# A feed-forward whose up projection goes by Strassen's block product and whose down projection goes in six groups

## The chip, the cores and the metric

The kernel is one program on one core of a Trainium2 chip. The metric is the device time of one execution in microseconds (us); each kernel is run several times and the median is given. PE is the matrix engine, DVE, ACT and POOL are the vector, scalar and general engines, SP issues the DMAs, all on one queue.

## The reference

Two trunk layers of width 1024 run over 640 tokens: 512 latent tokens (y_sample) and 128 context tokens (y_prompt), with shared weights. Each layer is a mixer of four branches (window attention, latent attention, pooling, gated delta rule) with a residual, and then a gated feed-forward:

```python
mod = jnp.matmul(jax.nn.silu(cond), lp['w_mod']) + lp['b_mod']
sh1, sc1, ga1, sh2, sc2, ga2 = jnp.split(mod[:, None, :], 6, axis=-1)
...
x = x + ga1 * rmsnorm(mix, lp['g_post1'])
h2 = rmsnorm(x, lp['g_pre2']) * (1 + sc2) + sh2
gt, up = jnp.split(jnp.matmul(h2, lp['w_up']), 2, axis=-1)
f = jnp.matmul(jax.nn.silu(gt) * up, lp['w_down'])
x = x + ga2 * rmsnorm(f, lp['g_post2'])
```

w_up is 1024 x 5632 (2816 gate and 2816 up columns), w_down 2816 x 1024. The change touches the three lines from h2 to f and what stands beside them in time.

## The kernel before, in words

All data are fp32. A product is made of two parts, hi (rounded to the matmul's format) and lo (the rest), and of three matmuls, hi x hi, hi x lo and lo x hi. Weights are split as they arrive: wchunk (L137) loads a tile of 128 x 1024 into "raw", ACT copies it to "whi" (L144) and DVE subtracts to get "wlo" (L145).

The activations h lie feature by token in hhi and hlo, 8 blocks of 128 features by 640 tokens, in two token halves of 384 and 256. The up projection takes 128 weight columns at a time (up_chunk, L1243): 8 blocks x 3 matmuls x 2 halves = 48 matmuls. There are 22 gate and 22 up chunks in a layer. ACT makes the Silu of the gate (L1291), DVE multiplies the up product in (L1293) and splits the result (L162).

The down projection goes in three groups of 8, 7 and 7 column blocks (FGROUPS) and two halves of 512 output columns, 660 matmuls of 512 columns in a layer. The sums of a group are added to y, in the tiles "acc" and "oh". The last half of the last group goes token tile by token tile (21 matmuls each): behind each tile stands post (L1219). It multiplies by the gate vector into a tile of "tg" (L1227), computes the norm's factor, adds both halves to the residual x in a tile of "V" with two scalar_tensor_tensor (L1232, L1233) and stores it (L1234). x was loaded into V beforehand (x_load, L1185); V, "tg", "cv" and "dt" have two buffers each. For layer 0 the tile then goes on into prenorm (L355), the norm that makes h of the next layer: transposes on PE, DVE scaling into P, hi on ACT (L378), lo on POOL or DVE (L380).

At the start of each feed-forward the norms of the last token tiles are late. ffn_head (L1246) runs four weight chunks over the first 384 tokens meanwhile.

In layer 0's feed-forward a filler computes the next layer's modulation (mod_group_v, L299) on DVE: 96 weight tiles of 128 x 512 with two operations each (L313, L315), whose raw tiles alternate between "dt" and "cv". step() issues one tile at a time between chunks.

Each engine runs its instructions in one fixed order, which a scheduler sets from the program's order and priorities when the kernel is built. An instruction that waits holds all behind it on its engine. Tiles of a tag share that tag's buffers, so a new tile waits until the readers of an old one are done.

Of the kernel before, what the change touches and what calls it, by code (L numbers as in the profile page):

```python
# [26 lines left out]
FGROUPS = ((0, 8), (8, 15), (15, 22))  # L27
# [77 lines left out]
class Step:  # L105
    def __init__(self, nc, tc, pools, I, O):
        self.nc, self.tc, self.I, self.O = nc, tc, I, O
        self.sb, self.psp, self.dr = pools
        self.n = 0
        self.late = []  # L110
        self.dma = nc.sync
        self.bg = None
# [5 lines left out]
    BUFS = dict(raw=2, whi=3, wlo=3, acc=4, tg=2, cv=2, oh=4, X=2, T=2, U=4, V=2, P=4, dt=2, st=4)  # L118
# [180 lines left out]
    def mod_group_v(self, M, g, bank, tr_tag):  # L299

        nc, I, l = self.nc, self.I, M["l"]
        pb = self.ps(bank)
        accs = []
        for j in range(4):
            acc = self.t("P", [128, SLOT])[:, :1024].rearrange("p (s c) -> p s c", s=2)
            accs.append(acc)
            for k in range(KT):
                raw = self.t("cv", [128, TG])[:, :512] if k % 2 else self.t("dt", [128, 512])
                c = g * 2048 + j * 512
                self.dma.dma_start(raw, I["w_mod"][l, k * 128:k * 128 + 128, c:c + 512])  # L310
# [12 lines left out]
        yield  # L323
# [31 lines left out]
    def prenorm(self, i, x, M, which, hh):  # L355
# [13 lines left out]
        for q in range(2):  # L369
# [849 lines left out]
    def post(self, i, t0, t1, s, G, xsrc, xdst, M, which, hh2):  # L1219
# [15 lines left out]
        if hh2 is not None:  # L1235
            norm = lambda: self.prenorm(i, x, M, which, hh2)
            if i < 3:
                norm()
            else:
                self.late.append(norm)  # L1240


    def up_chunk(self, l, c0, tags=("whi", "wlo")):  # L1243
        return self.wchunk([(slice(0, 128), self.I["w_up"][l][:, c0:c0 + 128].rearrange("(k p) c -> p k c", p=128))], KT, 128, tags)

    def ffn_head(self, l, hh):  # L1246

        head = {}
        for j, (n, up) in enumerate(((0, 0), (0, 1), (1, 0), (1, 1))):
            ch = self.up_chunk(l, up * D_FF + n * 128, ("whi", "wlo") if j < 3 else ("oh", "oh"))  # L1250
            p = self.ps("s" if up else "g")[:, :HV[0][1]]
            self.fm_h(ch, hh, outs=[p, None], halves=(0,))
            head[n, up] = ch, p
            if j in (0, 1):
                self.late.pop(0)()
        return head

    def ffn(self, l, hh, head, M, Mn, xsrc, xdst, hh2, filler):
        step = lambda: next(filler, None) if filler is not None else None
# [3 lines left out]
        G = None  # L1263
        for gi, (f0, f1) in enumerate(FGROUPS):
            nf = f1 - f0
            parts = {}
            for nm in ("hi", "lo"):
                if nm == "hi":
                    tl = [self.t("X", [128, 2 * SLOT], F32R)[:, :2560].rearrange("p (a t) -> p a t", a=4) for _ in range(2)]
                else:  # L1270
                    tl = [self.t(tg, [128, SLOT], F32R)[:, :1280].rearrange("p (a t) -> p a t", a=2)
                          for tg in ("T", "T", "U", "U")]
                per = 4 if nm == "hi" else 2
                parts[nm] = [tl[n // per][:, n % per, :] for n in range(nf)]
            for n in range(nf):
                gu = []
                for up in range(2):
                    bank = "s" if up else "g"
                    if gi == 0 and (n, up) in head:
                        ch, p = head[n, up]  # L1280
                        outs = [p, self.ps(bank)[:, :HV[1][1]]]
                        self.fm_h(ch, hh, outs=outs, halves=(1,))
                    else:
                        outs = self.fm_h(self.up_chunk(l, up * D_FF + (f0 + n) * 128), hh, bank)
                    gu.append(outs)
                    if n < nf - 1:
                        step()
                gp, up = gu
                s = self.t("tg", [128, TG])[:, :NTOK]
                for p, (o, sz) in zip(gp, HV):  # L1290
                    nc.scalar.activation(s[:, o:o + sz], p, AF.Silu)  # L1291
                for p, (o, sz) in zip(up, HV):
                    nc.vector.tensor_tensor(s[:, o:o + sz], s[:, o:o + sz], p, op=ALU.mult)  # L1293
                self.split(parts["hi"][n], parts["lo"][n], s)
            hs = (lambda k: parts["hi"][k], lambda k: parts["lo"][k])
            kc = [(k, min(k + 2, nf)) for k in range(0, nf, 2)]
            last = gi == len(FGROUPS) - 1
            for half in range(2):
                co = half * 512
                mk = lambda a, b: self.wchunk([(slice(0, 512), wd[:, f0 + a:f0 + b, co:co + 512])], b - a, 512)  # L1300
                if gi == 0 and half == 0:
                    for i in range(NT):
                        if i < 4:
                            ys.append(self.t("acc", [128, SLOT])[:, :1024])
                        else:
                            ys.append(self.t("oh", [128, SLOT])[:, :1024])
                if last and half == 1:
                    G = self.load_G(M, 1)
                    for i in range(NT):
                        y = ys[i][:, :512]  # L1310
                        nc.gpsimd.tensor_tensor(y, y, G[0 if i < 4 else 1][:, 0:512], op=ALU.mult)  # L1311
                    chs = [mk(a, b) if b - a == 2 else self.wchunk1(wd[:, f0 + a:f0 + b, co:co + 512]) for a, b in kc]
                    for i in range(NT):
                        p = self.ps("g")
                        for ci, (a, b) in enumerate(kc):
                            self.tmm(p, chs[ci], range(b - a), hs, range(a, b), i, ci == 0, ci == len(kc) - 1)
                        y = ys[i]
                        nc.vector.tensor_tensor(y[:, 512:], y[:, 512:], p, op=ALU.add)
                        self.post(i, y[:, :512], y[:, 512:], self.ffs[i], G, xsrc, xdst, Mn, 0, hh2)
                else:  # L1320
# [12 lines left out]
                    if last:  # L1333
                        self.ffs = []
                        for i in range(NT):
                            s = self.t("o_s2", [128, 2], bufs=6)
                            j = self.t("tg", [128, TG])[:, :NTOK]
                            nc.scalar.activation(j[:, :512], ys[i][:, :512], AF.Square, accum_out=s[:, 0:1])  # L1338
                            self.ffs.append(s)


    def run(self):
# [29 lines left out]
        for l in range(DEPTH):  # L1372
# [42 lines left out]
            hh = self.new_h()  # L1415
# [44 lines left out]
```

## Time and profile before

| | us |
|---|---|
| median of 3 runs (2438.87 to 2442.44) | 2440.92 |
| the profiled execution | 2436.05 |
| its span | 2433.9 |
| PE busy in it | 2349.3 (97%) |
| DVE busy | 1351.3 (56%) |
| ACT busy | 833.6 (34%) |
| POOL busy | 270.2 (11%) |

The mean granted clock of PE was 0.992 of full speed. Busy times of engines overlap, and matmuls are pipelined: the time from one start to the next is the price of one, not its length. In the records an idle time before an instruction stands in brackets with what ended it.

### The profile page before, as it was taken

How to read it: one execution, taken by the hardware profiler on the slowest of the kernel's cores; microseconds unless marked ns; L12 is line 12 of the kernel's file. 1: busy time of each engine (PE TensorE's matmuls, PEld its weight loads, DVE VectorE, ACT ScalarE, POOL GpSimd, SP SyncE). 2: the span in 40 equal slices, each digit the busy share in tenths (PEclk: the TensorE clock that was granted, in tenths of full speed). 3: DMA queues.
4: the chain of work that ended last, by engine and by line, in shares of the span. 5: the costliest groups of instructions: out<-in, count | busy, mean ns of one | idle time of the engine just before them, and what ended most of it. 6: DMA issues, size and time to landing. Idle time of an engine off the chain costs nothing.

```text
span 2433.9 us, 38640 instructions
## 1 busy us (share of the span) xinstructions
PE 2349.3 (97%) x15350; PEld 2084.1 (86%) x15350; DVE 1351.3 (56%) x2920; ACT 833.6 (34%) x1682; POOL 270.2 (11%) x324
## 2 busy tenths in 40 slices
PE   7999999999998999999989999999999999999998
PEld 5877688989877989989969777898898799899996
DVE  5562788576358746473285647874764553223225
ACT  3341554232235222212264534522422442222222
POOL 0000203132031000000020011221311200000001
PEclk9999999999999999999999999999999999999999
DMA  8637123424445636352243121242353332222223
GB/s 258 162 122 228 40 75 97 107 59 114 137 135 170 185 113 190 111 168 74 77 128 100 29 63 54 88 109 76 88 164 99 120 122 78 87 78 70 78 74 100
DMA packets 361668, 269.45 MB, mean 111 GB/s; under 512 B 72128, under 2 KB 312384, under 8 KB 361488
## 3 DMA queue, kind: packets, MB, share of 16 engines
q1 hardware_dynamic: 361488, 266.98, 37.4%
q8 instruction: 121, 1.98, 0.3%
q14 instruction: 59, 0.48, 0.1%
HBM read 234.73 MB, written 32.20 MB: 110 GB/s over the span
## 4 chain that ended last, share of the span: by engine, by line
PE 77%; DVE 11%; DMA 4%; ACT 3%; issue 2%; POOL 1%; SPq 1%; DVEq 0%; ACTq 0%; POOLq 0%
PE psg L129 39%; PE pss L129 24%; PE pso L129 4%; PE psc L129 4%; PE pst L129 2%; PE pst L134 2%; DVE wlo L145 1%; DVE P L990 1%; DVE P L989 1%; ACT whi L144 1%; PE psc L212 1%; DMA V<-in_w_mod 1%; DMA tg<-gd 1%; POOL acc L1177 1%; DMA gd<-tg 0%
## 5 line engine op out<-in xcount | busy, mean ns | idle before, releaser
L129 PE MATMUL psg<-hhi,whi 128*128 128x384 f32 (+1 forms) x2144 | 683.6, 319 | 13.4 <-ACT hhi L378 6.6
L129 PE MATMUL psg<-hlo,whi 128*128 128x384 f32 (+1 forms) x2144 | 681.5, 318 | 3.8 <-POOL hlo L380 3.8
L129 PE MATMUL psg<-hhi,wlo 128*128 128x384 f32 (+1 forms) x2144 | 679.0, 317 | 2.2 <-DVE wlo L145 2.0
L145 DVE TENSOR_TENSOR wlo<-raw,whi 128x1024 fp32r<-128x1024 f32 (+1 forms) x260 | 320.3, 1233 | 458.5 <-ACT whi L144 455.6
L144 ACT ACTIVATE whi<-raw 128x1024 fp32r<-128x1024 f32 (+1 forms) x260 | 272.3, 1049 | 672.2 <-PE psg L129 289.9
L129 PEld LDWEIGHTS psg<-hhi,whi 128*128 128x128 f32 x2144 | 406.2, 189 | 30.2 <-issue 8.4
L129 PEld LDWEIGHTS psg<-hlo,whi 128*128 128x128 f32 x2144 | 406.4, 190 | 20.3 <-issue 13.4
L129 PEld LDWEIGHTS psg<-hhi,wlo 128*128 128x128 f32 x2144 | 406.8, 190 | 12.9 <-issue 6.6
L129 PE MATMUL pss<-hhi,wlo 128*128 128x384 f32 (+1 forms) x672 | 208.1, 310 | 0.0
L129 PE MATMUL pss<-hhi,whi 128*128 128x384 f32 (+1 forms) x672 | 208.1, 310 | 0.0
L129 PE MATMUL pss<-hlo,whi 128*128 128x384 f32 (+1 forms) x672 | 208.1, 310 | 0.0
L1293 DVE TENSOR_TENSOR tg<-tg,pss 128x384 f32<-128x384 f32 (+1 forms) x88 | 42.8, 486 | 159.9 <-PE pss L129 159.9
L129 PEld LDWEIGHTS pss<-hhi,wlo 128*128 128x128 f32 x672 | 126.5, 188 | 0.0
L129 PEld LDWEIGHTS pss<-hlo,whi 128*128 128x128 f32 x672 | 126.5, 188 | 0.0
L129 PEld LDWEIGHTS pss<-hhi,whi 128*128 128x128 f32 x672 | 126.4, 188 | 0.0
L129 PE MATMUL psg<-oh,whi 128*128 128x384 f32 (+1 forms) x512 | 119.8, 317 | 4.8 <-DVE tg L1175 4.5
L1144 ACT ACTIVATE tg<-psg 128x384 f32<-128x384 f32 (+1 forms) x128 | 54.9, 431 | 188.9 <-PE psg L129 170.4
L1177 POOL TENSOR_TENSOR acc<-acc,tg 128x640 f32<-128x640 f32 x48 | 83.4, 1741 | 243.4 <-DVE tg L1175 243.3
L1311 POOL TENSOR_TENSOR acc<-acc,oh 128x512 f32<-128x512 f32 x8 | 12.8, 1602 | 857.5 <-ACT tg L1338 857.5
L129 PEld LDWEIGHTS psg<-oh,whi 128*128 128x128 f32 x512 | 85.3, 188 | 13.4 <-DVE tg L1175 8.4
L129 PE MATMUL psg<-wlo,X 128*128 128x512 f32 x224 | 88.8, 397 | 0.0
L129 PE MATMUL psg<-whi,X 128*128 128x512 f32 x224 | 87.5, 394 | 0.0
(488 smaller groups left out, 3985.5 us busy)
## 6 DMA issues: line engine op xcount, KB each, us to landing
raw<-in_w_up SPq DMA_DIRECT2D x88, 512.0 KB
raw<-in_w_in SPq DMA_DIRECT2D x86, 512.0 KB
raw<-in_w_down SPq DMA_DIRECT2D x40, 512.0 KB
V<-in_w_mod SPq DMA_DIRECT2D x32, 512.0 KB
cv<-in_w_mod SPq DMA_DIRECT2D x48, 256.0 KB
dt<-in_w_mod SPq DMA_DIRECT2D x48, 256.0 KB
raw<-in_w_o SPq DMA_DIRECT2D x16, 512.0 KB
xs<-V SPq DMA_DIRECT2D x15, 512.0 KB
```

The lines of the kernel that those rows point to most:

```text
L129: return self.nc.tensor.matmul(out, lhsT, rhs, start=start, stop=stop, skip_group_check=True)
L134: return self.nc.tensor.transpose(out, in_, self.ident[base:base + k, base:base + k])
L144: nc.scalar.activation(hi, raw[:, :a * b], AF.Copy)
L145: nc.vector.tensor_tensor(lo, raw[:, :a * b], hi, op=ALU.subtract)
L212: ins = f()
L989: nc.vector.tensor_tensor(t, bc(U[:104, 0:j, j], 2, n), bc(U[:104, j, j + 1:], 1, j), op=ALU.mult)
L990: nc.vector.tensor_tensor(U[:104, 0:j, j + 1:], U[:104, 0:j, j + 1:], t, op=ALU.add)
L1144: self.nc.scalar.activation(tg[:, o:o + sz], p, AF.Tanh, scale=0.5)
L1177: nc.gpsimd.tensor_tensor(a, a, tg, op=ALU.add)
L1293: nc.vector.tensor_tensor(s[:, o:o + sz], s[:, o:o + sz], p, op=ALU.mult)
L1311: nc.gpsimd.tensor_tensor(y, y, G[0 if i < 4 else 1][:, 0:512], op=ALU.mult)
```

## The change

For 256 weight columns the product of a 1024 x 256 weight tile and h is cut into blocks: features in two halves of 512, weight columns in two of 128, tokens in two of 320 (TH). In place of the eight block products, of 12 matmuls each, come seven of sums and differences of blocks (PRODUCTS 1, 5, 6, 2, 7, 3, 4; the form is Winograd's). The weight sums and differences are made on DVE for each 256 columns (up_pair, L1321 and on; its DVE operations have line L1333 in the records), and each of the seven operands is split hi and lo. The token side is made once per layer by combine. Products 1, 6, 7 and 4 accumulate in one PSUM tile X, which ACT copies out on the way; products 2, 5 and 3 are added by DVE. The head of the feed-forward is now products 1 and 2 of three column blocks, 72 matmuls. The down projection goes in six groups of 2, 4, 4, 4, 4 and 4 blocks; the last group takes both halves in one loop over token tiles, 24 matmuls each, with its single weight chunks in the buffers "tg" and "cv". The filler's raw tiles lie in V; step comes once after each 256 columns and three times per down chunk.

```diff
-FGROUPS = ((0, 8), (8, 15), (15, 22))
+FGROUPS = ((0, 2), (2, 6), (6, 10), (10, 14), (14, 18), (18, 22))
+TH = NTOK // 2
+PRODUCTS = 1, 5, 6, 2, 7, 3, 4
+HEAD = 1, 2, 5, 6, 3, 7, 4
...
-    BUFS = dict(raw=2, whi=3, wlo=3, acc=4, tg=2, cv=2, oh=4, X=2, T=2, U=4, V=2, P=4, dt=2, st=4)
+    BUFS = dict(raw=3, whi=3, wlo=3, acc=4, tg=2, cv=2, oh=4, X=2, T=2, U=4, V=2, P=4, dt=2, st=4)
...
-    def wchunk1(self, src):
+    def wchunk1(self, src, tags):
...
-        w = self.t("oh", [128, SLOT], F32R)[:, :1024].rearrange("p (a c) -> p a c", a=2)
...
+        hi, lo = (self.t(t, [128, TG], F32R)[:, :512] for t in tags)
...
-                raw = self.t("cv", [128, TG])[:, :512] if k % 2 else self.t("dt", [128, 512])
+                raw = self.t("V", [128, SLOT])[:, :512]
...
+    def combine(self, i, h32, hb):
...
+        def parts(p, t):
+            hi, lo = hb[p]
+            nc.scalar.activation(hi[:, :, dst], t, AF.Copy)
+            sub(lo[:, :, dst], t, hi[:, :, dst])
+
+        sub(t5, b12, hb[1][0][:, :, dst])
+        sub(t5, t5, hb[1][1][:, :, dst])
+        parts(5, t5)
+        sub(t6, b22, t5)
+        parts(6, t6)
+        sub(t5, b22, b12)
+        parts(7, t5)
+        sub(t6, hb[2][0][:, :, dst], t6)
+        sub(t6, t6, hb[2][1][:, :, dst], ALU.add)
+        parts(4, t6)
+
+    def up_pair(self, l, c0, hb, silu, E, order, tag="raw"):
...
+        def operand(p):
+            nonlocal s1
+            if p == 5 or p in (6, 7, 3) and 5 not in done:
+                s1 = self.t("dt", [128, 512]).rearrange("p (k c) -> p k c", k=4)
+                tt(s1, A21, A22, ALU.add)
+                done.add(5)
+            if p in (6, 7, 3) and 6 not in done:
+                tt(A21, A11, A21, ALU.subtract)
+                tt(A11, s1, A11, ALU.subtract)
+                done.add(6)
+            if p == 3:
+                tt(A12, A12, A11, ALU.subtract)
+            src = {1: A11, 2: A12, 3: A12, 4: A22, 5: s1, 6: A11, 7: A21}[p]
...
+            nc.scalar.activation(hi, src, AF.Copy)
+            tt(lo, src, hi, ALU.subtract)
+            return hi, lo
...
+            out = {2: Y, 5: Z, 3: Z}.get(p, X)
+            for k in range(4):
+                for y, (a, b) in enumerate(((whi, hhi), (whi, hlo), (wlo, hhi))):
+                    self.mm(out, a[:, k, :], b[:, k, :], p in (1, 2, 5) and k == 0 and y == 0, k == 3 and y == 2)
+            if p == 1:
+                nc.scalar.copy(eA[:, t1], X)
...
+            elif p == 2:
+                tt(eA[:, t1], eA[:, t1], Y, ALU.add)
...
+    def ffn_head(self, l, hb):
...
+        for j, (n, up) in enumerate(((0, 0), (0, 1), (1, 0))):
+            E = self.pair_tiles(n, up)
+            g = self.up_pair(l, up * D_FF + n * 256, hb, not up, E, HEAD, ("raw", "U", "V")[j])
+            head[n, up] = g, E
+            next(g)
+            next(g)
+            if late:
+                late.pop(0)()
...
+            chs = [[(mk(k, co), (0, 1), (k, k + 1)) for k in range(0, nf, 2)] for co in (0,)]
+            chs.append([(mk(0, 512), (0, 1), (0, 1))])
+            chs[1] += [(self.wchunk1(wd[:, f0 + k:f0 + k + 1, 512:1024], ("tg", "cv")), (0,), (k,)) for k in range(2, nf)]
+            for i in range(NT):
+                s = self.t("o_s2", [128, 2], bufs=6)
+                for half in range(2):
+                    p = self.ps("g")
+                    for j, (ch, kw, kh) in enumerate(chs[half]):
+                        self.tmm(p, ch, kw, hs, kh, i, j == 0, j == len(chs[half]) - 1)
+                    y = ys[i][:, half * 512:half * 512 + 512]
+                    nc.vector.tensor_tensor(y, y, p, op=ALU.add)
...
+                self.post(i, ys[i][:, :512], ys[i][:, 512:], s, G, xsrc, xdst, Mn, 0, hh2)
```

The order of the instructions moves with it. First DVE in layer 0, where the up projection of the first groups runs beside the filler. wlo, whi and raw are weight tiles (an operand's hi and lo now share one tile, whi or wlo by turns), P the filler's sum, pss a product of the up projection. Before:

```order
L145 TENSOR_TENSOR wlo_8145<-raw_8142,whi_8144 128x1024
L162 TENSOR_TENSOR T_7854<-tg_7999,X_7852 128x640
L315 SCALAR_TENSOR_TENSOR P_8062<-dt_8198,cs_218,P_8062 128x512 x2
L315 SCALAR_TENSOR_TENSOR P_8062<-cv_8202,cs_218,P_8062 128x512 x2
L315 SCALAR_TENSOR_TENSOR P_8062<-dt_8262,cs_218,P_8062 128x512 x2
L315 SCALAR_TENSOR_TENSOR P_8062<-cv_8266,cs_218,P_8062 128x512 x2
L145 TENSOR_TENSOR wlo_8209<-raw_8206,whi_8208 128x1024
L313 TENSOR_SCALAR P_8333<-dt_8334,cs_218 128x512 x2
L315 SCALAR_TENSOR_TENSOR P_8333<-cv_8338,cs_218,P_8333 128x512 x2
L1293 TENSOR_TENSOR tg_8135<-tg_8135,pss_8077 128x384
```

And now, in a gate and up pair of group 2 (L319 and L321 are the filler):

```order
L1333 TENSOR_TENSOR raw_9052<-raw_9052,raw_9050 128x4x128
L321 SCALAR_TENSOR_TENSOR P_8945<-V_9002,cs_218,P_8945 128x512 x2
L1333 TENSOR_TENSOR oh_9049<-oh_9049 128x320
L321 SCALAR_TENSOR_TENSOR P_8945<-V_9006,cs_218,P_8945 128x512 x2
L1333 TENSOR_TENSOR whi_9143<-raw_9052,whi_9143 128x512
L1333 TENSOR_TENSOR wlo_9159<-raw_9052,wlo_9159 128x512
L321 SCALAR_TENSOR_TENSOR P_8945<-V_9010,cs_218,P_8945 128x512 x2
L1333 TENSOR_TENSOR oh_9049<-oh_9049,pss_9076 128x320
L319 TENSOR_SCALAR P_9177<-V_9178,cs_218 128x512 x2
L1333 TENSOR_TENSOR whi_9191<-raw_9187,whi_9191 128x512
L1333 TENSOR_TENSOR dt_9208<-raw_9187,raw_9189 128x512
```

Between two filler tiles there stood one operation of the weights or of the product per 128 columns; now there stand up to three weight operations, of half the size, and an add.

Next DVE at the very end of layer 1, the last two token tiles. psg is the sum of a tile's matmuls, tg the product by the gate vector, V the residual. Before:

```order
L1232 SCALAR_TENSOR_TENSOR V_22580<-acc_19973,rr_22586,V_22580 128x512
L1233 SCALAR_TENSOR_TENSOR V_22580<-tg_22583,rr_22586,V_22580 128x512
L1318 TENSOR_TENSOR oh_19974<-oh_19974,psg_22601 128x512
L1227 TENSOR_TENSOR tg_22627<-oh_19974,oh_22395 128x512
L1230 TENSOR_TENSOR ss_22631<-o_s_3311_22390 128x1
```

And now, from the last tile's first add on (L1481 are the adds of psg, L1238 the products into tg, L1244 the second step into V):

```order
L1481 TENSOR_TENSOR oh_19726<-oh_19726,psg_23313 128x512
L245 SCALAR_TENSOR_TENSOR rr_23297<-rs_u_23301,rr_23297 128x1
L1238 TENSOR_TENSOR tg_23135<-acc_19722,oh_23066 128x512
L1238 TENSOR_TENSOR tg_23188<-acc_19723,oh_23066 128x512
L1244 SCALAR_TENSOR_TENSOR V_23132<-tg_23135,rr_23138,V_23132 128x512
L1244 SCALAR_TENSOR_TENSOR V_23185<-tg_23188,rr_23191,V_23185 128x512
L1238 TENSOR_TENSOR tg_23241<-acc_19724,oh_23066 128x512
L1238 TENSOR_TENSOR tg_23294<-acc_19725,oh_23066 128x512
L1481 TENSOR_TENSOR oh_19726<-oh_19726,psg_23330 128x512
```

Before, a tile's product stood right behind its add; now the products of all tiles stand behind the first add of the last tile.

Last SP's queue at the same place, the stores of the results and the loads of x (xs) into V. Before:

```order
L1234 DMA out_y_sample<-V_22448 128x1024
L1185 DMA V_22536<-xs 128x1024
L1234 DMA out_y_sample<-V_22492 128x1024
L1185 DMA V_22580<-xs 128x1024
L1234 DMA out_y_sample<-V_22536 128x1024
L1185 DMA V_22624<-xs 128x1024
L1234 DMA out_y_sample<-V_22580 128x1024
L1234 DMA out_y_prompt<-V_22624 128x1024
```

And now:

```order
L1245 DMA out_y_sample<-V_23132 128x1024
L1245 DMA out_y_sample<-V_23185 128x1024
L1196 DMA V_23238<-xs 128x1024
L1196 DMA V_23291<-xs 128x1024
L1245 DMA out_y_sample<-V_23238 128x1024
L1245 DMA out_y_sample<-V_23291 128x1024
L1196 DMA V_23344<-xs 128x1024
L1245 DMA out_y_prompt<-V_23344 128x1024
```

Before, stores and loads alternated from the first tile on; now two stores stand ahead of two loads, twice.

## Rows read from the trace of the kernel before

**Rows 1.** The page: busy time of each engine, its share and instructions.
```profile
PE 2349.3 (97%) x15350; PEld 2084.1 (86%) x15350; DVE 1351.3 (56%) x2920; ACT 833.6 (34%) x1682; POOL 270.2 (11%) x324
```

**Rows 2.** Windows: busy us and count by engine, granted clock, DMA share, GB/s.
```profile
756.00:768.00 12.00, 8.23 (x35) 7.37 (x34) 11.94 (x33) 8.44 (x15) 1.81 (x1) 0.86 0.70 225
893.00:960.00 67.00, 67.00 (x334) 57.59 (x334) 53.86 (x80) 16.99 (x23) 0.00 (x0) 1.00 0.71 219
1232.00:1260.00 28.00, 23.71 (x111) 18.05 (x110) 27.04 (x89) 19.62 (x38) 5.68 (x11) 1.00 0.57 175
1986.00:2200.00 214.00, 214.00 (x1311) 203.09 (x1311) 56.36 (x65) 53.58 (x74) 0.00 (x0) 1.00 0.26 79
```

**Rows 3.** Timeline of PE, up projection: start, length, engine, line, operation.
```profile
949.74 0.34 PE L129 MATMUL pss<-hhi,whi 128*128 128x384 f32 x1
...
952.38 0.28 PE L129 MATMUL pss<-hhi,whi 128*128 128x256 f32 x1
...
955.22 0.34 PE L129 MATMUL psg<-hhi,whi 128*128 128x384 f32 x1
```

**Rows 4.** Timeline of PE, last matmuls of layer 1.
```profile
2418.16 0.39 PE L129 MATMUL psg<-whi,X 128*128 128x512 f32 x1
...
2421.43 0.40 PE L129 MATMUL psg<-whi,U 128*128 128x512 f32 x1
...
2422.13 0.40 PE L129 MATMUL psg<-oh,U 128*128 128x512 f32 x1
```

**Rows 5.** Timeline of DVE, start of layer 0's feed-forward.
```profile
756.58 0.15 DVE L1230 TENSOR_TENSOR ss<-o_s 128x1 f32<-128x1 f32 x1
756.65 1.22 DVE L145 TENSOR_TENSOR wlo<-raw,whi 128x1024 fp32r<-128x1024 f32 x1
...
781.91 0.39 DVE L376 TENSOR_SCALAR P<-psc,modA,modB 128x128 f32<-128x128 f32 x1
...
785.54 0.68 DVE L380 TENSOR_TENSOR hlo<-P,hhi 128x512 fp32r<-128x512 f32 x1
786.14 0.74 DVE L315 SCALAR_TENSOR_TENSOR P<-dt,cs,P 128x512 f32<-128x512 f32 x1
...
788.13 0.54 DVE L1293 TENSOR_TENSOR tg<-tg,pss 128x384 f32<-128x384 f32 x1
788.60 0.47 DVE L313 TENSOR_SCALAR P<-dt,cs 128x512 f32<-128x512 f32 x1
...
794.12 0.82 DVE L162 TENSOR_TENSOR T<-tg,X 128x640 fp32r<-128x640 f32 x1
...
795.99 1.41 DVE L315 SCALAR_TENSOR_TENSOR P<-dt,cs,P 128x512 f32<-128x512 f32 x2
```

**Rows 6.** Timeline of PE, waits in the heads of layers 0 and 1.
```profile
759.74 0.44 PE L129 MATMUL psg<-hhi,whi 128*128 128x384 f32 x1 [2.49 <-ACT hhi L378]
...
785.12 0.38 PE L129 MATMUL psg<-hlo,whi 128*128 128x256 f32 x1 [1.09 <-POOL hlo L380]
...
1951.30 0.45 PE L129 MATMUL psg<-hhi,whi 128*128 128x384 f32 x1 [2.46 <-ACT hhi L378]
...
1974.09 0.39 PE L129 MATMUL psg<-hlo,whi 128*128 128x256 f32 x1 [0.16 <-POOL hlo L380]
```

**Rows 7.** Timelines of SP's queue and of DVE, end of layer 1.
```profile
2408.78 0.36 SPq L1234 DMA_DIRECT2D out_y_sample<-V  x1
2413.50 0.33 SPq L1185 DMA_DIRECT2D V<-xs  x1
...
2430.21 0.34 SPq L1234 DMA_DIRECT2D out_y_prompt<-V  x1
...
2417.74 0.75 DVE L1232 SCALAR_TENSOR_TENSOR V<-acc,rr,V 128x512 f32<-128x512 f32 x1 [1.14 <-DMA V<-xs]
...
2429.43 0.75 DVE L1233 SCALAR_TENSOR_TENSOR V<-tg,rr,V 128x512 f32<-128x512 f32 x1
```

**Rows 8.** Waits of PE, 1215 to 1320: total us, times, longest.
```profile
PE psg L129 <- POOL hlo L380: 1.8, 1, 1.8
```

More of the change, by code (lines that the diff above doesn't have):

```diff
@@ L110, in __init__ @@
         self.late = []
+        self.wn = 0
+        self.h32 = {}
+        self.quarter = None
         self.dma = nc.sync
@@ L377, in prenorm @@
             ks = slice(4 * q, 4 * q + 4)
+            if which:
+                continue
             nc.scalar.activation(hh[0][:, ks, sl], h32[:, ks], AF.Copy)
@@ L1236, in post @@
             norm = lambda: self.prenorm(i, x, M, which, hh2)
-            if i < 3:
+            if which == 0:
+                if i < 3:
+                    norm()
+                else:
+                    self.late.append(norm)
+            elif i < 2:
                 norm()
-            else:
-                self.late.append(norm)
-    def up_chunk(self, l, c0, tags=("whi", "wlo")):
-        return self.wchunk([(slice(0, 128), self.I["w_up"][l][:, c0:c0 + 128].rearrange("(k p) c -> p k c", p=128))], KT, 128, tags)
@@ L1246, in ffn_head @@
-    def ffn_head(self, l, hh):
-        head = {}
[L1249 to L1255, printed above, removed]
-        return head
-    def ffn(self, l, hh, head, M, Mn, xsrc, xdst, hh2, filler):
-        step = lambda: next(filler, None) if filler is not None else None
+            elif i == 2:
+                h32 = norm()
+                self.late.append(lambda: (self.more_hb(hh2), self.combine(i, h32, hh2)))
+            else:
+                self.late.insert(2 * i - 6, lambda: self.h32.__setitem__(i, norm()))
+                self.late.append(lambda: self.combine(i, self.h32.pop(i), hh2))
@@ new lines, in norm_blocks @@
+    def norm_blocks(self, i, h32, hb):
+        nc = self.nc
+        for a, b in ((i * 128, min(i * 128 + 128, TH)), (max(i * 128, TH), i * 128 + 128)):
+            if a >= b:
+                continue
+            second = a >= TH
+            src, dst = slice(a - i * 128, b - i * 128), slice(a - TH * second, b - TH * second)
+            for q in range(2):
+                if second and q == 0:
+                    continue
+                hi, lo = hb[3 if second else 1 + q]
+                v = h32[:, 4 * q:4 * q + 4, src]
+                nc.scalar.activation(hi[:, :, dst], v, AF.Copy)
+                eng = nc.gpsimd if q == 0 else nc.vector
+                eng.tensor_tensor(lo[:, :, dst], v, hi[:, :, dst], op=ALU.subtract)
@@ new lines, in pair_tiles @@
+    def pair_tiles(self, n, up):
+        if n % 2 == 0:
+            return [self.t(("tg", "cv")[up], [128, TG])[:, :NTOK] for _ in range(2)]
+        e = self.t("oh", [128, SLOT])
+        return [e[:, :NTOK], e[:, NTOK:2 * NTOK]]
+    def ffn_head(self, l, hb):
+        head = {}
+        late = self.late
+        self.late = []
+        for j, (n, up) in enumerate(((0, 0), (0, 1), (1, 0))):
[6 more added lines that the diff above has]
+                late.pop(0)()
+        while late:
+            late.pop(0)()
+        return head
@@ L1260, in ffn, with step @@
+    def ffn(self, l, hb, head, M, Mn, xsrc, xdst, hh2, filler):
+        def step(k=1):
+            for _ in range(k if filler is not None else 0):
+                next(filler, None)
         nc, I = self.nc, self.I
@@ L1262, in ffn @@
         ys = []
-        G = None
+        t1, t2 = slice(0, TH), slice(TH, NTOK)
         for gi, (f0, f1) in enumerate(FGROUPS):
             nf = f1 - f0
[L1266 to L1276, printed above, removed]
-                for up in range(2):
[L1278 to L1282, printed above, removed]
-                    else:
[L1284 to L1294, printed above, removed]
-            hs = (lambda k: parts["hi"][k], lambda k: parts["lo"][k])
[L1296 to L1320, printed above, removed]
```

118 lines of the change are left out of this document (103 added, 15 removed).

## The prediction

> **What bounds the kernel now.** I read the busy times of the page first. PE is busy 2349.3 of 2433.9 us [rows 1], so the span is PE time plus some 85 us of waits. The windows by stage say where those waits are [rows 2]. In layer 0's feed-forward (893 to 960) and in layer 1's (1986 to 2200) PE is busy all of the time at granted clock 1.00. In the first of these two DVE is busy 53.9 of 67 us, because the filler runs there; in the second it is busy 56.4 of 214. So the feed-forward is PE-bound, with much spare DVE time in layer 1 and little where the filler runs. The waits lie at its edges: 756 to 768, where the feed-forward begins (PE 8.2 of 12 us), and 1232 to 1260, where layer 0 passes to layer 1 (23.7 of 28).
>
> The timeline of PE gives the price of a matmul as the step from one start to the next, since the ends overlap. Fifteen of 384 columns start between 949.74 and 952.38, 0.176 us each, and 24 of 256 columns between 952.38 and 955.22, 0.1183 each [rows 3]. Fourteen of 512 columns take 2418.16 to 2421.43, 0.2336 each [rows 4]. A control: in layer 1 the last blocks of h arrive at 1974.1 [rows 6]. What is left then is 44 chunks x 24 x (0.176 + 0.1183) = 310.8 us less the head's 4 x 24 x 0.176 = 16.9, and 660 down matmuls x 0.2336 = 154.2. That gives 2422.2; the trace's last matmul starts at 2422.13 and lasts 0.40 [rows 4]. The sums of PE steps hold.
>
> **1. The matmuls saved.** For 256 columns of w_up, 96 matmuls (48 of each width, 14.13 us) become 84 of 320 columns. No row has 320 columns. Between the two neighbours it is 0.1472, and 84 of them take 12.36 us. The bounds are 0.118 and 0.176, the neighbours themselves; I take the middle because 512 columns lie on the same line (0.1183 + 256 x 0.00045 = 0.2335). Over 44 column blocks the saving is 77.6 us, 38.8 in each layer. The down projection keeps its 660 matmuls a layer.
>
> A sentence apart: the Trainium skill (TensorE: Matmul & The Clock Gate, Part 1, "Wait — 56ns, not 53.3ns?") gives a start-to-start spacing of columns divided by 2.4 GHz plus about 2.5 ns, which for 320 columns would be 0.136 us and a saving of 119 us in all. By that rule 384 columns would take 0.1625 where the rows show 0.176, so the trace does not agree and the measurement decides.
>
> **2. The head.** Before, PE does 16.9 us of head work while the late token tiles are normed, and the late half starts at 786.0 (785.12 and the clock's recovery) in layer 0 and at 1974.1 in layer 1 [rows 6]. After, product 5 needs combine() of tiles 2, 3 and 4, and up to there PE has only 72 matmuls, 10.6 us. I price the DVE instructions in their new order from the first weight lo to the last hlo of product 5. A DVE step is its record less some 0.075 us (785.54 lasts 0.68, the next starts at 786.14) [rows 5]: 0.60 for 512 elements, 0.40 for 320 (between 0.34 for 256 and 0.47 for 384), 0.34 for 256, 0.67 for scalar_tensor_tensor of 512, 0.32 for the 128-column norm step. So 32 x 0.60 + 12 x 0.34 + 3 x 0.40 + 4 x 0.67 + 10 x 0.32 + 33 one-column steps of about 0.1 = 34 us. DVE begins at 756.65 [rows 5], which gives 790.7; for the ACT hi copies between and the pair whose weights go through V, I add 4.3 (bounds 2 and 10): product 5 at 795. In layer 1 the same 38 us from 1948.2, three us ahead of the first matmul at 1951.30 [rows 6], end at 1987. From there (1848 - 72) x 0.1472 = 261.4 us of up projection are left. Layer 0: 786.0 + 293.9 against 795 + 261.4, 23.5 us gained. Layer 1: 1974.1 + 293.9 against 1987 + 261.4, 19.6 gained. Of 77.6 us the heads take 34.5, and 43.1 are left.
>
> **3. DVE in layer 0.** A gate and up pair takes PE 168 x 0.1472 = 24.7 us. DVE has for it 14 lo and 8 combinations of 512 elements (13.2 us), 6 adds of 320 (2.4), the product (1.5) and the split (1.5): 18.6 us. In layer 1 this fits below PE, and I charge only 3 us in all for ACT and DVE replies between products. In layer 0 the filler comes on top. In the new DVE order the stretch from the second pair of group 1 to the end of group 3 holds 133 scalar_tensor_tensor (88.2), 20 tensor_scalar at 0.40 (8.0), 109 operations of 512 (65.4), 40 of 320 (16.0), 20 y adds (12.0), 9 lo of 1024 at 1.15 (10.3), 15 of 640 at 0.74 (11.1) and 2 us of small ones: 213 us. PE has five pairs and two down groups of 120 matmuls there, 5 x 24.7 + 2 x 28.0 = 179.5. So DVE sets the pace for about 33 us. Before, a pair of the same weights cost DVE 4 x 1.15 + 2 x (0.47 + 0.34) + 2 x 0.74, 7.7 us, and the filler fitted. The filler's raw tiles now use V's two buffers in place of four; a wait for one holds all weight work queued behind it on DVE. I add 5 us. Together 38; the bounds are 0 (in the stage before DVE has 30 us of work beside 35 of PE, and this lead with slack that I don't see swallows it) and 60 (DVE and PE wait for each other in turn).
>
> The same stretch raises the clock. In 1232 to 1260 PE was busy 85% with waits of up to 1.8 us, and the granted clock stayed at 1.00 [rows 2, 8]; in 756 to 768, after a wait of 2.49 us, it was 0.86 on the mean [rows 2, 6]. Here PE would be busy 179.5 / 213, 84%, in short gaps, so I charge nothing. The Trainium skill (same page, "HAM oscillation — how this bites in real kernels") warns that idle gaps between groups of matmuls put the clock back to half rate; this stretch at 1.2 GHz would take PE twice 179.5 us, far over DVE's 213. By the first of these two rows that doesn't happen with gaps of this size; it stays in the slow rival below.
>
> **4. The last group's tile loop.** The weights of two column blocks now lie in both buffers of "tg", and post() takes its product from "tg" too. In the new DVE order all five products L1238 stand after the last tile's matmuls; before, each stood behind its own tile. Let E be the last matmul's end (before 2422.5). Before, the last product step ends at 2429.43 + 0.75 and the span at 2433.9, E + 11.4 [rows 4, 7]. After, from E: products and steps for tiles 0 and 1, outputs issued at E + 2.2. V has two buffers, so x of tiles 2 and 3 is loaded when those outputs have landed: 2408.78 to 2413.50, 4.7 us, and it is usable 4.24 us later [rows 7]: E + 11. Two tiles' steps, outputs at E + 12 to 13; tile 4's x is asked for at E + 16.6 and usable at E + 20.9; its two steps end at E + 22.3, and 3.7 us from there to the end as before: E + 26. Cost 14.6 us (bounds 8, if DVE reaches the first outputs sooner, and 20).
>
> **5. From layer 0 to layer 1.** The same loop feeds the next norms. Before, the first projection matmul comes among the last tiles' posts, and the waits in 1215 to 1320 are small (1.8 us the longest) [rows 8]. After, tile 0's h can be there some 9 us after E, tiles 2 and 3 at about E + 20 and tile 4 at E + 29, through the same V round trip. The projection has some 5.4 us of PE work per tile to fill with (24 matmuls of 496 columns, 0.226 by the line of step 1). Some 11 us idle against 5 before: 6 us, bounds 0 and 12.
>
> **Sum.** 43.1 - 38 - 3 - 14.6 - 6 = -18.5: slower. The profiled execution took 2436.05 us, so 2454.6; the median shown is 4.9 above that execution, so about **2459 us**.
>
> **Rivals.** *Faster: DVE's excess is hidden.* The whole of step 3 is a sum of DVE steps against a sum of PE steps; where buffers let DVE run ahead in layer 0's first groups and PE catch up in the last ones, the 33 + 5 us vanish. For it: DVE has 213 us only if each step costs what it did beside PE's reads. Against it: three raw buffers and three of each weight tag hold under two products' lead (1.77 us each). Then 43.1 - 3 - 14.6 - 6 = 19.5 gained: 2421.
>
> *No change.* Half of step 3 is hidden: 2459 - 19 = 2440.
>
> *Much slower: the adds in DVE's queue.* Each add of a product (L1333, 320 columns) waits for PE, and lo operands that PE needs next are queued behind it. In layer 0, where DVE is already late, PE then waits for DVE and DVE for PE. 30 adds and 10 products by one product's 0.7 us of PE tail is 28 us on top, 2487; with the half clock it is more. Decisive from the point where DVE holds no product ready when PE begins one. For it: before, DVE's waits for the up products (L1293) cost nothing because nothing behind them was late, and now it is; against it: the new order puts one to three weight steps ahead of most adds.
>
> *No saving:* a matmul of 320 columns costs like 384 (its weight load would bind). 84 x 0.176 is 14.8, more than before; but 256 columns at 0.118 exclude it nearly.
>
> **Chances and range.** Forecast 0.50 (2446 to 2478), hidden excess 0.20, no change 0.13, much slower 0.15, no saving 0.02. Less than 0.2%, 4.9 us, can't be told from no change. Faster 0.21, same 0.13, slower 0.66. The range reaches into the faster and the much slower rival: 2418 to 2488.
>
> **What would show it.** PE's busy time falls by about 78 us and the steps of 320 columns are 0.147; PE idles 15% between about 850 and 1060 at granted clock 1.00, ended by DVE lo tiles (L1333), with DVE over 90% busy; layer 1's middle is PE-bound; product 5 starts 9 to 13 us later than h was complete before; from last matmul to end 26 us. Wrong if layer 0's middle shows PE at 98% or more (the faster rival), or if layer 1's middle also falls below 95%.

## The result and the profile after

The changed kernel took 2467.5 us (median of 4, 2463.9 to 2471.4), the kernel before 2440.1 in the same series: ratio 1.0111, 95% interval 1.0094 to 1.0129. The forecast was 2459, with a range of 2418 to 2488, and slower.

The page of the changed kernel answers to [rows 1]:

```profile
PE 2305.1 (93%) x14822; PEld 2027.0 (82%) x14822; DVE 1670.7 (68%) x3546; ACT 998.5 (40%) x2076; POOL 259.4 (11%) x320
```

PE is busy 44 us less and not the 78 that were forecast, though the span is 36 us longer. Before the missing 34 are looked for, the price of a matmul. The timeline of PE in layer 1 (start, length, engine, line, operation):

```profile
2143.51 1.92 PE L135 MATMUL psg<-X,wlo 128*128 128x320 f32 x12
2145.28 0.31 PE L135 MATMUL pss<-hhi,whi 128*128 128x320 f32 x1
```

Twelve matmuls of 320 columns take 1.77 us, 0.1475 each: the middle of its neighbours, as forecast. So the matmuls that are left cost what they should, and "busy" holds something else: matmuls at the lower clock, where one of 320 columns lasts 0.47 us (862.18, below) and not 0.31. The windows by stage show it (the columns as in [rows 2]; the granted clock is the third figure from the end, 0.70 in the first row):

```profile
768.00:800.00 32.00, 15.85 (x69) 13.50 (x68) 29.25 (x73) 19.13 (x37) 0.00 (x0) 0.70 0.20 66
850.00:900.00 50.00, 39.15 (x215) 35.62 (x214) 48.27 (x79) 18.42 (x32) 0.00 (x0) 0.86 0.53 169
900.00:950.00 50.00, 39.58 (x188) 30.84 (x187) 43.82 (x73) 7.65 (x14) 0.00 (x0) 0.91 0.49 152
1250.00:1300.00 50.00, 38.91 (x160) 30.51 (x159) 36.69 (x98) 24.99 (x49) 9.64 (x15) 0.86 0.43 125
2100.00:2150.00 50.00, 50.00 (x278) 45.30 (x277) 29.52 (x44) 17.23 (x29) 0.00 (x0) 1.00 0.27 85
```

Three stages have lost PE time: the head (768 to 800), layer 0's feed-forward while the filler runs (850 on, DVE busy 48 of 50 us), and the passage to layer 1 (1250 to 1300). In all three the clock is below 1.00 too. Layer 1's feed-forward is PE-bound at full clock.

Where the time went is read from landmarks that both traces have: the same norm's transposes ahead of each head, and the first rope of layer 1. Before:

```profile
754.78 0.66 PE L134 MATMUL pst<-cst,P 128*128 128x128 f32 x4 [1.43 <-ACT P L363]
1298.27 0.91 PE L129 MATMUL pst<-P,T 128*128 128x384 f32 x2 [0.29 <-DVE P L593]
1946.34 0.66 PE L134 MATMUL pst<-cst,P 128*128 128x128 f32 x4 [1.44 <-ACT P L363]
```

And after, with a wait in the head (776.88), the first matmul of product 5 in each layer (797.09, 2031.86) and the last matmuls of each feed-forward (1277.73, 2447.02):

```profile
758.96 0.66 PE L140 MATMUL pst<-cst,P 128*128 128x128 f32 x4 [1.44 <-ACT P L369]
776.88 1.12 PE L140 MATMUL pst<-cst,P 128*128 128x128 f32 x4 [5.86 <-ACT P L369]
797.09 0.41 PE L135 MATMUL pss<-hhi,wlo 128*128 128x320 f32 x1 [2.45 <-ACT hhi L1307]
1277.73 0.40 PE L135 MATMUL psg<-tg,U 128*128 128x512 f32 x1
1286.23 1.11 PE L140 MATMUL pst<-cst,P 128*128 128x128 f32 x4 [8.10 <-ACT P L369]
1290.37 0.78 PE L135 MATMUL psg<-whi,hhi 128*128 128x496 f32 x1 [2.17 <-ACT hhi L386]
1290.94 0.61 PE L135 MATMUL psg<-wlo,hhi 128*128 128x496 f32 x1
1343.28 0.91 PE L135 MATMUL pst<-P,T 128*128 128x384 f32 x2 [0.29 <-DVE P L604]
1992.92 0.66 PE L140 MATMUL pst<-cst,P 128*128 128x128 f32 x4 [1.44 <-ACT P L369]
2031.86 0.64 PE L135 MATMUL pss<-hhi,wlo 128*128 128x320 f32 x1 [2.44 <-ACT hhi L1307]
2447.02 0.40 PE L135 MATMUL psg<-tg,U 128*128 128x512 f32 x1
```

| stretch | before | after | difference | forecast |
|---|---|---|---|---|
| to the head of layer 0 | 754.8 | 759.0 | +4.2 | 0 |
| layer 0's feed-forward and the passage | 543.5 | 584.3 | +40.8 | +22 |
| layer 1's mixer | 648.1 | 649.6 | +1.5 | 0 |
| layer 1's feed-forward | 476.2 | 454.5 | -21.7 | -18.1 |
| last matmul's end to the end | 11.4 | 22.2 | +10.8 | +14.6 |
| sum | | | +35.6 | +18.5 |

The profiled execution after was the slowest of its four (2471.4) and that before lay 4 us under its median; by medians the difference is 27.4 us. The first stretch, where nothing was changed but the raw buffers, moved by -6 to +5 us from one kernel's trace to the next, and is counted as scatter.

### The profile page after: what moved, and what is told of

The parts are those of the page before. It is cut to its first block, busy times and chain, and to the rows that moved or that the text cites. A ratio compares the mean times of both kernels' runs of the same rounds, so it can differ in the third digit from the quotient of the medians.

```text
span 2469.6 us, 38694 instructions
## 1 busy us (share of the span) xinstructions
PE 2305.1 (93%) x14822; PEld 2027.0 (82%) x14822; DVE 1670.7 (68%) x3546; ACT 998.5 (40%) x2076; POOL 259.4 (11%) x320
## 5 line engine op out<-in xcount | busy, mean ns | idle before, releaser
L135 PE MATMUL psg<-hhi,wlo 128*128 128x384 f32 (+2 forms) x1632 | 509.8, 321 | 9.4 <-ACT wlo L1352 4.4
L135 PE MATMUL psg<-hhi,whi 128*128 128x384 f32 (+2 forms) x1600 | 502.3, 321 | 7.1 <-DVE tg L1186 5.6
L135 PE MATMUL psg<-hlo,whi 128*128 128x384 f32 (+2 forms) x1520 | 486.9, 320 | 0.0
L151 DVE TENSOR_TENSOR wlo<-raw,whi 128x1024 fp32r<-128x1024 f32 (+1 forms) x170 | 212.7, 1252 | 177.7 <-ACT whi L150 175.0
L135 PEld LDWEIGHTS psg<-hhi,whi 128*128 128x128 f32 x1600 | 300.9, 190 | 20.6 <-issue 8.1
L135 PEld LDWEIGHTS psg<-hlo,whi 128*128 128x128 f32 x1520 | 288.5, 190 | 16.2 <-issue 14.3
L135 PE MATMUL pss<-hhi,whi 128*128 128x320 f32 x512 | 133.9, 330 | 29.0 <-ACT whi L1352 13.4
L135 PE MATMUL pss<-hhi,wlo 128*128 128x320 f32 x544 | 134.1, 314 | 7.6 <-ACT hhi L1307 4.9
L321 DVE SCALAR_TENSOR_TENSOR P<-V,cs,P 128x512 f32<-128x512 f32 x168 | 119.2, 749 | 16.8 <-DMA V<-in_w_mod 16.3
L135 PEld LDWEIGHTS pss<-hhi,whi 128*128 128x128 f32 x512 | 94.6, 202 | 34.1 <-DVE whi L1333 15.1
L135 PE MATMUL psg<-whi,U 128*128 128x512 f32 x356 | 117.2, 392 | 0.0
L1333 DVE TENSOR_TENSOR wlo<-raw,wlo 128x512 fp32r<-128x512 f32 x118 | 81.2, 689 | 47.7 <-ACT wlo L1352 47.1
L1333 DVE TENSOR_TENSOR whi<-raw,whi 128x512 fp32r<-128x512 f32 x122 | 83.6, 689 | 29.3 <-ACT whi L1352 29.3
```

The costliest lines, as they stand in the source:

```text
L135: return self.nc.tensor.matmul(out, lhsT, rhs, start=start, stop=stop, skip_group_check=True)
L151: nc.vector.tensor_tensor(lo, raw[:, :a * b], hi, op=ALU.subtract)
L1333: tt = lambda o, x, y, op: nc.vector.tensor_tensor(o, x, y, op=op)
```

## The experiments

Ratios are to the kernel before, run on the same chip in the same series (its medians there were 2435.3 to 2440.1); they lie up to 0.0012, 3 us, from the quotients of the medians. A stretch of layer 0 is measured in the one traced execution of each kernel. The theory (A): the filler makes DVE the bound in layer 0, and tg's two buffers make the tail and the passage. The rivals: the products' own replies stop PE (B), or the six groups do (C).

**The filler left out in part.**

```diff
+                if k > 0:
+                    if k % 2 and (j, k) != (3, KT - 1):
+                        yield
+                    continue
                 raw = self.t("V", [128, SLOT])[:, :512]
```

> The changed kernel with the filler's k loop cut to its first step: 12 of 96 weight tiles are loaded and multiplied on DVE in layer 0's feed-forward, 84 are left out (the next layer's modulation is then not the reference's). Theory A (the filler makes DVE the bound of layer 0's feed-forward): from product 5 to the last down matmul of layer 0 the 481 us of the changed kernel fall to 416 to 425, the PE sum, granted clock 1.00 there; time 2467 - 60 = 2405 to 2415. Rival B (ACT, DVE and PSUM replies between the seven products stop PE, the filler only stands in the same time): the stretch stays above 455 and the time above 2440.

Measured 2404.0, ratio 0.9856 (0.9826 to 0.9886), 62 us under the changed kernel by the ratios. The windows of its trace, the same stretches of layer 0:

```profile
788.00:1211.00 423.00, 422.14 (x2496) 388.13 (x2496) 290.46 (x473) 187.91 (x339) 5.80 (x12) 0.99 0.30 93
850.00:1000.00 150.00, 149.91 (x896) 136.39 (x896) 103.43 (x172) 60.20 (x107) 0.00 (x0) 1.00 0.32 103
```

From product 5 to the last down matmul it takes 423 us, where the PE sum is 415.6, some 60 matmuls of the modulation come on top, and the changed kernel took 481, 58 us more. PE idles 0.9 us, and from 850 to 1000 the clock is at 1.00. Theory A holds here, and B falls: the seven products by themselves stop PE no more than in layer 1. The run drops the loads of the filler together with its DVE work, so it doesn't part DVE's sum from the waits for V.

**The filler stretched over four groups.**

```diff
-                        step(3)
+                        step(2)
```

> The changed kernel with step(2) in place of step(3) per down chunk, so that the filler lies over four groups and not three; the same work. Theory A (DVE's excess is local: 213 us of DVE beside 180 of PE): per group of two pairs and a down projection DVE has about 80 us beside 77.5 of PE, so the excess falls from 33 to some 10 us and the gaps of PE, and the half clock with them, mostly go: 2467 - 35 to 50 = 2417 to 2432. Rival B (what stops PE is each reply, not the pace): within 8 us of the changed kernel.

Measured 2442.0, ratio 1.0019 (1.0004 to 1.0035): 22 us off, between the two expectations: less than A expected and more than B. The excess is one of pace, as A says, but PE still idles 24.4 us from product 5 to the last down matmul, 457 us in all, where the changed kernel idled 40.8 of 481. The windows, first of the changed kernel and then of this run:

```profile
797.00:1278.00 481.00, 440.19 (x2496) 394.95 (x2496) 396.74 (x642) 187.33 (x340) 5.79 (x12) 0.97 0.41 128
```

```profile
792.00:1249.00 457.00, 432.58 (x2496) 394.88 (x2496) 392.71 (x642) 185.60 (x340) 5.80 (x12) 0.97 0.42 134
850.00:900.00 50.00, 41.43 (x224) 38.02 (x223) 47.24 (x76) 19.13 (x33) 0.00 (x0) 0.86 0.53 167
900.00:950.00 50.00, 46.26 (x273) 41.47 (x272) 46.91 (x81) 17.25 (x34) 0.00 (x0) 0.97 0.40 129
1000.00:1050.00 50.00, 46.18 (x316) 43.92 (x315) 48.46 (x84) 25.19 (x49) 0.00 (x0) 1.00 0.40 130
```

In 900 to 950 and in 1000 to 1050 PE is busy some 6 us more than in the changed kernel (39.58 and 40.49); the 50 from 850 on are nearly as they were. A single wait of 6.7 us stands there, the longest of this stage. In the changed kernel's timelines it looks like this, DVE first and then the matmuls that wait:

```profile
860.28 0.69 DVE L1333 TENSOR_TENSOR dt<-raw,raw 128x512 f32<-128x512 f32 x1
860.88 2.74 DVE L321 SCALAR_TENSOR_TENSOR P<-V,cs,P 128x512 f32<-128x512 f32 x4
863.53 0.82 DVE L168 TENSOR_TENSOR U<-oh,U 128x640 fp32r<-128x640 f32 x1
864.27 0.69 DVE L1333 TENSOR_TENSOR whi<-dt,whi 128x512 fp32r<-128x512 f32 x1
```

```profile
861.75 0.64 PE L135 MATMUL pss<-hhi,whi 128*128 128x320 f32 x1 [6.81 <-ACT whi L1352]
862.18 0.47 PE L135 MATMUL pss<-hlo,whi 128*128 128x320 f32 x1
865.01 0.90 PE L135 MATMUL pss<-hhi,whi 128*128 128x320 f32 x2 [1.83 <-DVE whi L1333]
```

ACT's hi is named as what PE waited for, but ACT could start it only when DVE's sum (860.28) was done, and that sum stood in DVE's queue behind group 0's filler. The lo that follows stands behind four more filler operations (860.88).

**The product of post in T.**

```diff
-        j = self.t("tg", [128, TG])[:, :512]
+        j = (self.t("tg", [128, TG]) if which else self.t("T", [128, SLOT]))[:, :512]
```

> The changed kernel with the product of the feed-forward's post in a tile of T (free by then) in place of tg. Theory (tg's two buffers, held by the last weights, put all products behind the last tile): end of layer 1 as before, last matmul to span end 11 to 13 us in place of 22.2, and PE's idle time between layer 0's last down matmul and the next projection (8.1 + 2.2 us and a stretch at half clock) falls to about 5: 2467 - 10 - 8 to 14 = 2443 to 2449. Rival (V's two buffers alone cause it, the round trip of 8 to 9 us per tile): tail stays above 18 us, time within 6 us of the changed kernel.

Measured 2440.8, ratio 1.0011 (1.0000 to 1.0021), 24 us off. The end of the changed kernel, DVE and SP's queue:

```profile
2446.77 2.19 DVE L1238 TENSOR_TENSOR tg<-acc,oh 128x512 f32<-128x512 f32 x2 [1.06 <-PE psg L135]
2456.26 0.75 DVE L1243 SCALAR_TENSOR_TENSOR V<-acc,rr,V 128x512 f32<-128x512 f32 x1 [1.59 <-DMA V<-xs]
2464.50 0.75 DVE L1243 SCALAR_TENSOR_TENSOR V<-oh,rr,V 128x512 f32<-128x512 f32 x1 [4.77 <-DMA V<-xs]
```

```profile
2449.65 1.01 SPq L1245 DMA_DIRECT2D out_y_sample<-V  x2
2452.38 1.58 SPq L1196 DMA_DIRECT2D V<-xs  x2
2457.71 2.39 SPq L1245 DMA_DIRECT2D out_y_sample<-V  x2
2460.38 0.33 SPq L1196 DMA_DIRECT2D V<-xs  x1
2465.95 0.33 SPq L1245 DMA_DIRECT2D out_y_prompt<-V  x1
```

And with the product in T, the last matmul, the last step and the last store (span 2440.7):

```profile
2430.02 0.39 PE L135 MATMUL psg<-tg,U 128*128 128x512 f32 x1
```

```profile
2436.22 0.74 DVE L1244 SCALAR_TENSOR_TENSOR V<-T,rr,V 128x512 f32<-128x512 f32 x1
```

```profile
2436.99 0.34 SPq L1245 DMA_DIRECT2D out_y_prompt<-V  x1
```

The tail is 10.3 us in place of 22.2, and from layer 0's last down matmul to layer 1's first rope it is 50.6 in place of 65.2. The rival (V's two buffers alone) falls. The norms of the tile loop now begin ahead of the last down matmul, and from product 5 to that matmul it takes 486.7 us in place of 481.0.

**The kernel before with six groups.**

```diff
-FGROUPS = ((0, 8), (8, 15), (15, 22))
+FGROUPS = ((0, 2), (2, 6), (6, 10), (10, 14), (14, 18), (18, 22))
```

> The kernel before with the six groups of the changed one (2, 4, 4, 4, 4, 4 blocks) and nothing else: no block product, the old last half by token tile. Theory A (the groups are paid on DVE by 30 more y adds a layer, which have cover where PE is the bound): 2440, within 6 us. Rival C (the six groups themselves cost, by adds that hold up PSUM banks and by shorter groups): 2455 or more, and so a good part of the loss of the changed kernel.

Measured 2442.1, ratio 1.0011 (0.9996 to 1.0025). By the medians it is 5.5 us, by the ratio at most 6. C, which needed 15 us or more, falls.

**Both edits, the filler even** (step(2 if gi and k == 0 else 1), and the product in T).

> The changed kernel with two edits: post's product in a tile of T, and the filler spread over all groups (once per down chunk in group 0, then 2 and 1 in turn: 10 steps of 2.65 us per group, so DVE has some 74 us beside 77.5 of PE). If pace is what makes PE wait in layer 0 (theory A), both gains add: from product 5 to the last down matmul 481 falls to 416 to 428, the tail to 11 to 13 us; ratio to before 0.975 to 0.985, about 2380 to 2400. If the two edits share their gain (rival: a shorter tile loop only moves the wait into the next projection, or the late filler collides with it), the ratio stays above 0.992.

Measured 2409.0, ratio 0.9873 (0.9857 to 0.9890): 58 us under the changed kernel. The gains add: the two single edits gave 22 and 24, and the more even spacing gives some 12 more (from product 5 to the last down matmul 445.7 us, where step(2) alone had 457.2). But the expected range was missed: that stretch was to fall to 416 to 428. So 22 us of the 58 that the filler cost are still there against the thinned kernel's 423, a part of them the norms of the tile loop, as with the product in T alone.

**x of two tiles in X as well** (x_load of tiles 1 and 3 into a tile of "X").

> As the kernel with both edits, and the residual x of token tiles 1 and 3 loaded into a tile of X (free by then), so that four buffers take x in place of two. If V's two buffers still cost a round trip of 8 to 9 us in the tile loop, the tail shortens by 1 to 3 us and the passage to layer 1 by up to 5: ratio 0.001 to 0.003 under the kernel with both edits. If the products in tg were all of it, no difference within 0.001.

Measured 2407.5, ratio 0.9872 (0.9855 to 0.9889): no difference. Once the products are free, V's round trip costs nothing here that can be told.

**Both edits, V=3 and raw=2.**

> As the kernel with both edits, with three buffers of V and two of raw in place of two and three. If the two V buffers hold up the filler's tiles (DVE waits of 16.8 us for V in the changed kernel) and the posts in the head, 3 to 8 us less than with both edits alone; if the third raw buffer is what lets DVE and ACT make operands ahead, 5 us or more slower, with waits of PE for whi or wlo in layer 1 too, where the changed kernel has none.

Measured 2400.5, ratio 0.9839 (0.9820 to 0.9859), 8 us better, at the upper end of the first expectation. From 850 to 950 the clock no longer falls:

```profile
850.00:900.00 50.00, 49.34 (x271) 44.24 (x270) 47.10 (x76) 17.03 (x30) 0.00 (x0) 1.00 0.49 158
900.00:950.00 50.00, 47.27 (x323) 45.00 (x322) 42.03 (x75) 23.70 (x47) 0.00 (x0) 1.00 0.35 112
```

But that is not where the time went. From product 5 to the last down matmul it takes 446.4 us, as with both edits alone (445.7), and from the landmark ahead of layer 0's head to the end 1647.2 against 1648.8. The two traced executions lie 11.1 us apart, and 9.4 of that stand ahead of the landmark, in the stretch that was counted as scatter above. What V's third buffer gives on top of both edits is not shown.

**V=3 and raw=2 alone on the changed kernel.**

> The changed kernel with three buffers of V and two of raw, and nothing else. If the filler's tiles and the posts wait for V (16.8 us of DVE waits for V in layer 0, and the x round trips at both tile loops), the tails shorten by 4 to 8 us each and layer 0 by 5 to 10: 2445 to 2455, ratio 1.002 to 1.006. If V was no bound, within 4 us of the changed kernel, 1.010 to 1.013; PE's gaps and the clock of layer 0's feed-forward stay, since DVE's sum is the same.

Measured 2447.7, ratio 1.0047 (1.0030 to 1.0065), as expected if V binds. DVE's idle time ahead of the filler's operations (L321), nearly all of it for V's loads, falls from 16.8 to 5.6 us, from product 5 to the last down matmul it takes 471.1 us in place of 481.0, and the tail falls from 22.2 to 15.9; PE's clock in layer 0 stays low, 0.97 over 800 to 1250. So without the other edits V's two buffers cost some 10 us of the 58 in layer 0 and 6 of the tail.

**Two column blocks in the head.**

```diff
-        for j, (n, up) in enumerate(((0, 0), (0, 1), (1, 0))):
+        for j, (n, up) in enumerate(((0, 0), (0, 1))):
```

> The changed kernel with two column blocks in the head in place of three (48 matmuls of cover and not 72), and so without the weight tiles in V; everything else as it was. If DVE's queue sets the time of product 5 (38 us of it from the first weight lo), product 5 comes 3 to 6 us earlier, for DVE loses two lo, two sums and an add and waits for V's weights, and the time is within 4 us of the changed kernel, since 3.5 us of matmuls come later. If PE's cover sets it, product 5 doesn't move and the kernel loses 3 to 4 us in each layer, 2474.

Measured 2452.3, ratio 1.0058 (1.0036 to 1.0080): 13 us better, a miss on the time. The step named for product 5 was met: in its trace

```profile
784.38 0.63 PE L135 MATMUL pss<-hhi,wlo 128*128 128x320 f32 x1 [5.69 <-ACT hhi L1307]
```

it comes 33.0 us after the landmark (751.43 there) in place of 38.1, and 6.0 earlier in layer 1. So DVE's queue sets it and not PE's cover. By the landmarks layer 1's feed-forward gives 2.9 us and layer 0's 9. Whether what layer 0 gives beyond layer 1 comes from V, which the third block's weights occupied, the next run asks.

**All of it: V=3, raw=2, both edits and two blocks in the head; and with x in X.**

> The kernel with both edits and three V buffers (raw two), and two column blocks in the head in place of three. Alone on the changed kernel the shorter head took 13 us off. If that came from DVE's queue in the heads (product 5 some 5 us earlier after the first norm of the head, in both layers), about 2 to 3 us per layer remain here: ratio 0.980 to 0.983. If it came from the V buffers that the third block's weights hold, V's third buffer has given that already: ratio 0.983 to 0.986, no gain on the kernel with three V buffers.

Measured 2397.9, ratio 0.9845 (0.9823 to 0.9867): nothing gained on 0.9839. That fits with V's third buffer having given it already, but doesn't show it.

> As the kernel with two blocks in the head and three V buffers, and x of token tiles 1 and 3 in a tile of X. With three V buffers the round trip of x binds only tiles 3 and 4, so 0 to 2 us: ratio within 0.001 of the kernel without it.

Measured 2396.2, ratio 0.9840 (0.9825 to 0.9854), no difference. All versions with both edits beat both kernels. The simplest of the fastest has the filler even, post's product in T and three V buffers: 1.6% under the kernel before and 2.7% under the changed one.

## Why the prediction was right

**The matmuls saved** (step 1) were sized right, at 0.1475 against 0.1472 each.

**The heads** (step 2) were right in size and cause. Product 5 was put at 795 and 1987 on before's clock; less the landmarks' shifts it came at 797.1 - 4.2 = 792.9 and 2031.9 - 46.6 = 1985.3. In layer 1, 415.6 us follow from there to the last matmul's end, the 261.4 + 154.2 of the sum, so the 1.5 us for replies there were none.

**DVE in layer 0** (step 3) was right in its mechanism, which the thinned filler showed. Of the 481 us from product 5 to the last down matmul PE idles 40.8, where 33 + 5 + 1.5 were charged, and DVE is over 90% busy in the stretch that was named:

```profile
850.00:1060.00 210.00, 174.84 (x951) 152.13 (x950) 195.49 (x319) 64.54 (x116) 0.00 (x0) 0.93 0.50 158
```

The clock there is 0.93 and not 1.00. What failed is the sentence that gaps of 15% cost no clock, so that "I charge nothing". The mean clock was 0.97 from 797 to 850, 0.92 from 850 to 1000 and 0.99 from 1000 to 1115; 0.03 of 53, 0.08 of 150 and 0.01 of 115 us give some 15 us that the half clock took. The busy times agree: the same 2496 matmuls keep PE busy for 440.2 us here and for 422.1 in the thinned kernel. The row I leaned on, 1232 to 1260 of before [rows 2], had no wait over 1.8 us [rows 8]; here one of 6.8 came, and the matmuls behind it last 0.64 and 0.47 us where they last 0.31 at full clock. The share of busy time was the wrong measure. But the length of a wait alone doesn't settle it either: before, the clock was 0.98 from 786 to 893 behind waits of 1.67 and 1.09 us. The Trainium skill (TensorE: Matmul & The Clock Gate, "HAM oscillation — how this bites in real kernels") warns that a matmul group behind a long wait starts at the half clock. That was worth more than nothing here and less than the rival that I gave it: the trace agrees for twice those 15 us, some 30 of the 481, and not for the whole stretch.

**From layer 0 to layer 1** (step 5) I charged 6 us; it cost 15.1 (65.2 against 50.1). The windows of this passage, before and after:

```profile
1248.21:1298.27 50.06, 44.73 (x233) 37.90 (x233) 30.37 (x70) 26.04 (x46) 6.29 (x4) 1.00 0.50 136
```

```profile
1278.13:1343.28 65.15, 50.89 (x249) 42.31 (x249) 44.37 (x123) 35.26 (x64) 7.77 (x6) 0.90 0.51 147
```

PE idles 14.3 us where it idled 5.3, so 9 us more and not 6: the waits of 8.1 and 2.2 us, and 4 us in shorter ones that the sum left out. The other 6 us are longer busy time: 16 more transposes of the norms, which stood ahead of the last down matmul before, and again the clock. Matmuls of 496 columns last 0.61 us (1290.94) and from 1296.5 on 0.39. The half clock costs some 4 us there, an estimate from the 10 us of 1286.23 to 1296.5, of which 2.4 are waits.

Together these make the +40.8 of this stretch, 18.8 us over the +22 of the sum: the passage 9.1, and 11.8 from product 5 to the last down matmul (before, the same ground from 786.0 on took 462.2 us, 14.1 over its own PE sum), less 2.1 by which the head was cheaper.

**The tail** (step 4) was foreseen at E + 26 and came at E + 22.2: the store-and-load round trips were right in kind, and shorter. A store landed 2.7 us after its issue (2449.65 to 2452.38) where 4.7 had been read from 2408.78 to 2413.50 [rows 7]. Before, three such steps took 4.7 to 5.2 us, and with the product in T three took 2.6 to 3.2. Why they differ stays open.

Of the rivals, "much slower" lay nearest to what was missing, by its half clock. Its own mechanism is not what stopped PE: DVE's idle time for PE ahead of the adds (L1333 from pss) is 2.5 us in all from 797 to 1278, and 3.8 for ACT's copies, against the 28 that the rival gave it. "No change" and "hidden" needed a part of DVE's excess to be hidden; none was.

The forecast of 2459 came 8.5 us short of 2467.5, and a part of that nearness is luck: the stretch from layer 0's head to layer 1 was 18.8 us too low, and layer 1's feed-forward and the tail, 3.6 and 3.8 too high, took some of it back. By the medians the kernels lie 8 us closer together than in the two traces.

## What to carry to other kernels

A product with fewer matmuls moves work to the engines that prepare operands. Sum their steps stage by stage, with what runs beside them, before the saving is counted: here 78 us of PE were saved, and DVE's filler, crowded into three groups, took back some 60. When a chunk of weights is put into a tag of two buffers, look who else rotates through that tag up to the chunk's last use. And where a wait of several microseconds on PE appears, look at the granted clock behind it: here the half clock took some 15 us beside 41 us of idle time in layer 0.

## What had not been expected of the hardware

Around waits of 5.9, 6.8 and 8.1 us the granted clock of 32 to 50 us fell to 0.70 to 0.86. Shorter waits did both: a row with waits of up to 1.8 us stayed at 1.00, and behind waits of 1.67 and 1.09 us in the head of before the clock fell for a while (0.98 over 107 us).

With both edits and three V buffers PE is 95 to 99% busy at full clock from 850 to 950, beside a DVE that is busy 42 to 47 of each 50 us and with no wait of PE over 1.8 us. With the filler bunched, PE was 78 to 79% busy there beside a DVE that was busy 44 to 48. Over the whole of layer 0's feed-forward even the spaced filler still costs: 446 us where the thinned one takes 423.
